# Encoder block on one core: five buffer and order edits between its stages

## The chip, the core and the metric

The program runs on one core of one Trainium2 chip. The time is device time of one execution in microseconds (us); of several runs the median is given. The engines are TensorE (PE; its weight loads are listed apart as PEld), VectorE (DVE), ScalarE (ACT), GpSimd (POOL) and SyncE (SP). SP, ACT and POOL also issue DMAs, each through its own queue. Each engine works through its instructions in a fixed order and stands still at an instruction whose inputs or buffers are not ready.

## What is computed

One layer of a bidirectional encoder, applied to a request of 256 tokens and to one of 512, with the same weights, all in float32, model width 1024. Cut to what matters:

```python
h = rmsnorm(x)
u, q, k, v, qm, gl = split(h @ w_in)               # 8192 columns
A = z * sigmoid(z @ s5_w_glu)                      # z = gelu(forward + backward S5 scan of u + d * u)
B = diff_attention(q, k, v)                        # 8 heads, two softmax maps each, rotary, norms
C = memory_attention(qm, rmsnorm(mem))             # 4 heads, 256 memory tokens
merged = sum_n sigmoid(gl_n + b_n) * (branch_n @ w_branch_n)    # n = A, B, C
x = x + merged @ w_out
x = x + (silu(g) * up) @ w_down                    # g, up = rmsnorm(x) @ w_gate_up
```

## The kernel before

All 768 tokens are worked on together. A stage's activations lie in SBUF with the features on the partitions, as a pair of float32r tiles, a high part and the residual, and so do the weights. A product is three matmuls into one PSUM bank (`mm3`, L748 to L753: high by high, high by residual, residual by high), for 8 slices k of the inner width. `dense_fm` (L755) runs this for 128 output features and one of the two token segments `SEGS`, 256 or 512 tokens wide; `between`, if given, is called after each k.

Weights come as a stream (`WStream`, L504): each chunk of 256 output columns is loaded in two halves into three raw buffers (`wr`, pool `W.praw`) by SP, ACT rounds it to the high part `wh` (L595), and DVE subtracts for the residual `wl` (L601); in some stages ACT writes the negated raw values (L598) and an accumulating DMA from POOL adds (L599).

**Who sets the order.** The program is written as one sequence. A planner then orders each engine's instructions ahead of time, by program order among what its own time estimates hold for ready, and places the tiles. `pin` (`keep_in_program_order`) puts an instruction behind everything written before it for its engine. `issue_after(ins)` puts what a block writes for the engine of `ins` behind `ins` in that engine's order. A pool's tiles with one tag share `bufs` buffers; a pool opened where a closed one lay waits, tile by tile, for the last use of what lay there. Side work is written as generators that `Pace` (L802) steps by a rate as the main loop calls `tick`.

The stages, in order, with what the change touches:

- *Memory keys, values and queries* with the memory attention beside them; its outputs go to DRAM (`mo_scr`).
- *u* (`u_chunk`, L1063): 4 chunks of 256 features. Each of the two 128-feature halves m gets a tile `ut` (three border columns are cleared by POOL, L277), filled by DVE for the 256-token segment (L1075) and ACT for the 512-token one (L1073), and stored to DRAM by SP (L282). Chunks 2 and 3 use a pool of one buffer (L1090), while DVE and ACT prepare the S5 parameters.
- *Gate logits* (L1105): 12 chunks of 256. ACT copies each result with its bias (L1114), SP stores it (L1115). Beside it the S5 scan runs as a generator, `s5.steps` (L452), 16 quads of 4 groups, each in several steps: `build` (DVE products, and ACT copies L310), `response`, `weights` (transposes L357 with ACT copies L358), `tables` (12 ACT instructions L375 to L377, then sines), `states` (products L403, DVE L391 to L426) and `outputs`. There are two PSUM banks for the gate logits.
- *Queries, keys and values* of the differential attention (L1392): units of 128 tokens, 24 matmuls of 256 columns each, with the gelu of the S5 outputs (`gelu`, L1366) and `diff_attend` (L1246) beside. `stack(h, i)` (L1213) transposes head h's queries (i = 0) or keys (i = 1): two groups of transposes into the three banks of `env.psb`, copied out by ACT (L1232) and DVE (L1234, L1236); for the keys two DMAs from POOL follow (L1240). In the last units POOL loads the memory branch's input over the normed activations, in three thirds of 256 tokens (L1404).
- *Branch C* (`branch(2, ...)`, L1491, called at L1544): 4 chunks of 256 features, two halves m each. A gate tile is loaded by POOL (L1499) and goes through tanh on ACT (L1500); DVE multiplies it with each segment's result (L1506). The rest of the attention is stepped between the k slices. At chunk 3 (`tail`, L1532) the attention is drained, its pools are closed, and `x1` and then the z pair (L1540) are placed where they lay; `load_pair` (L1521) splits the stored z into the pair, ACT L745 and DVE L746. The last head's output tile `do` is filled by ACT (L1334) and stored from ACT's queue (L1335).
- *Half-GLU* (L1547), then branches A and B, then `w_out`.
- *Feed-forward*: gate and up blocks by a seven-product scheme with half-size operands, and the down projection likewise (L1695 on): products in the order P2, P1, P5, P6, P3, P7, P4, each of 6 granules g, 42 items. `w_fetch(i)` (L1731) loads a quarter of the down weights, in some products with an accumulating DMA from POOL behind it (L1754). `make(i)` (L1757) splits the weights (`whd` by ACT L742, `wld` by DVE L743), sums or subtracts two activation quarters on DVE (L1767; P5, P6, P3 and P7 only) and splits the result (`dxh` by ACT L745, `dxl` by DVE L746), all pinned. In iteration i the loop fetches item i + 6, makes item i + 2 and issues the 18 matmuls of item i; behind a product's last granule DVE adds the sums to `x1` (L1846).

## Time and profile before

| | |
|---|---|
| median of 3 runs | 1772.24 us |
| the runs | 1771.3 to 1774.49 us |
| the profiled execution | 1774.09 us |
| its span | 1772.3 us |
| mean granted TensorE clock | 0.997 |
| moved by DMA | 234.09 MB, mean 132 GB/s |

The profile's span runs from the first to the last instruction; about 1.8 us of the execution lie around it. "Busy" is the time in which an engine works on an instruction, weight loads listed apart. In the view of waits a row names the engine, operation and line that stood still, what released it, the total, the number of times and the longest. In the timeline a row has its start, its duration, engine, line, operation, output and inputs with their sizes, and in brackets how long the engine was idle before and what ended it. A row of the chain of waits has start, duration and what it was. In a table by stretches each stretch has its length, the busy time of PE, PEld, DVE, ACT and POOL, the granted TensorE clock, the busy share of the DMA engines and their GB/s.

```profile
PEclk9999999999999999999999999999999999999999
DMA  7223745655556456444773336331312323239765
```

These two rows give the span in 40 equal slices, in tenths: the granted clock, and the share in which the DMA engines are busy, high at the start and again near the end, in the down projection.

### The profile page before, as it was taken

Reading aid. Unit: us, or ns where it says so; the run is one execution under the profiler, and the core shown is the slowest. Engines: PE = TensorE matmul, PEld = TensorE weight load, DVE = VectorE, ACT = ScalarE, POOL = GpSimd, SP = SyncE. Lnnn points to the kernel's source line nnn. Section 1 sums busy time; section 2 is a strip of 40 time slices with the busy share of each in tenths; the row PEclk is TensorE's granted clock in tenths of the full one; section 3 lists DMA queues with packets and bytes.
Section 4 is the critical chain, followed back from the end, with each engine's and each line's share of the span. In section 5 each row is a group of like instructions: output and inputs, shape, how many; then the busy total and the mean of one; then the engine's idle time right before and its main releaser. Section 6 shows DMA issues by size and latency. Waiting matters only on the chain.

```text
span 1772.3 us, 29415 instructions
## 1 busy us (share of the span) xinstructions
PE 1743.5 (98%) x11194; PEld 1609.4 (91%) x11194; DVE 1268.0 (72%) x2349; ACT 887.5 (50%) x1856; POOL 277.0 (16%) x296
## 2 busy tenths in 40 slices
PE   9999999999999999999989999999999999999998
PEld 9999988999999999999979888888889999998876
DVE  6665659699999679788876435453598777776775
ACT  6445444676676356877766434232343333334333
POOL 0000000000000101110110002000036565641112
PEclk9999999999999999999999999999999999999999
DMA  7223745655556456444773336331312323239765
GB/s 266 73 84 98 141 111 120 175 129 146 146 141 159 130 151 172 107 97 95 158 174 103 119 125 238 121 116 60 92 58 90 117 86 114 90 125 284 191 159 120
DMA packets 209661, 234.09 MB, mean 132 GB/s; under 512 B 57832, under 2 KB 173296, under 8 KB 209520
## 3 DMA queue, kind: packets, MB, share of 16 engines
q1 hardware_dynamic: 184080, 164.05, 30.6%
q0 software_dynamic: 24288, 65.02, 17.1%
q10 hardware_dynamic: 1152, 3.15, 0.5%
q8 instruction: 88, 1.44, 0.3%
q14 instruction: 53, 0.43, 0.1%
HBM read 165.78 MB, written 41.22 MB: 117 GB/s over the span
## 4 chain that ended last, share of the span: by engine, by line
PE 57%; DMA 3%; DVE 2%; issue 1%; ACT 1%; POOL 0%; SPq 0%; ACTq 0%; POOLq 0%; DVEq 0%
PE br L751 3%; PE br L752 3%; PE br L753 3%; PE gate L751 3%; PE gate L753 3%; PE up L753 3%; PE gate L752 3%; PE up L752 3%; PE up L751 3%; PE dn L751 3%; PE dn L752 3%; PE dn L753 3%; PE av L1311 2%; PE qk L752 2%; PE qk L751 2%; PE qk L753 2%
## 5 line engine op out<-in xcount | busy, mean ns | idle before, releaser
L595 ACT ACTIVATE wh<-wr 128x1024 fp32r<-128x1024 f32 x124 | 140.6, 1134 | 75.7 <-PE br L752 31.0
L601 DVE TENSOR_TENSOR wl<-wr,wh 128x1024 fp32r<-128x1024 f32 x82 | 108.4, 1324 | 84.7 <-ACT wh L595 82.9
L751 PE MATMUL gl<-Hhi,wh 128*128 128x256 f32 (+1 forms) x384 | 133.1, 346 | 2.4 <-ACT glt L1114 2.4
L753 PE MATMUL gl<-Hhi,wl 128*128 128x256 f32 (+1 forms) x384 | 129.7, 338 | 0.0
L752 PE MATMUL gl<-Hlo,wh 128*128 128x256 f32 (+1 forms) x384 | 129.4, 337 | 0.0
L751 PE MATMUL qk<-wh,Hhi 128*128 128x256 f32 x384 | 108.8, 283 | 0.7 <-ACT V L1210 0.7
L752 PE MATMUL qk<-wl,Hhi 128*128 128x256 f32 x384 | 109.4, 285 | 0.0
L753 PE MATMUL qk<-wh,Hlo 128*128 128x256 f32 x384 | 108.6, 283 | 0.0
L599 POOL DMA_DIRECT2D wl<-wr x42 | 36.6, 872 | 455.5 <-ACT wl L598 428.6
L751 PE MATMUL dn<-whd,dxh 128*128 128x512 f32 x231 | 89.2, 392 | 4.8 <-ACT dxh L745 4.8
L752 PE MATMUL dn<-wld,dxh 128*128 128x512 f32 x231 | 88.7, 390 | 0.0
L753 PE MATMUL dn<-whd,dxl 128*128 128x512 f32 x231 | 82.0, 390 | 0.6 <-DVE dxl L746 0.6
L751 PEld LDWEIGHTS gl<-Hhi,wh 128*128 128x128 f32 x384 | 73.0, 190 | 9.8 <-ACT glt L1114 2.8
L753 PEld LDWEIGHTS gl<-Hhi,wl 128*128 128x128 f32 x384 | 72.7, 189 | 7.9
L752 PEld LDWEIGHTS gl<-Hlo,wh 128*128 128x128 f32 x384 | 73.1, 190 | 7.2
L1280 DVE TENSOR_REDUCE nm<-sc 128x1 f32<-128x512 f32 (+1 forms) x96 | 56.5, 597 | 26.2 <-PE sc L1275 25.3
L751 PEld LDWEIGHTS qk<-wh,Hhi 128*128 128x128 f32 x384 | 73.2, 191 | 1.6 <-ACT V L1210 0.9
L557 ACT ACTIVATE wh_S<-ws 128x512 fp32r<-128x512 f32 x70 | 41.1, 625 | 65.5 <-PE up L752 36.9
L753 PEld LDWEIGHTS qk<-wh,Hlo 128*128 128x128 f32 x384 | 73.5, 191 | 0.3
L752 PEld LDWEIGHTS qk<-wl,Hhi 128*128 128x128 f32 x384 | 73.0, 190 | 0.6
L558 DVE TENSOR_TENSOR wl_S<-ws,wh_S 128x512 fp32r<-128x512 f32 x70 | 57.9, 850 | 15.9 <-ACT wh_S L557 15.9
L1282 ACT ACTIVATE p<-sc,nm 128x512 f32<-128x512 f32 (+1 forms) x96 | 59.0, 619 | 17.4 <-DVE nm L1280 17.0
(480 smaller groups left out, 6001.4 us busy)
## 6 DMA issues: line engine op xcount, KB each, us to landing
wr<-in_w_in_dram SPq DMA_DIRECT2D x48, 512.0 KB, 4.6
wr<-in_w_gate_up_dram SPq DMA_DIRECT2D x44, 512.0 KB, 3.5
wl<-wr POOLq DMA_DIRECT2D x42, 512.0 KB, 5.1
wr<-in_w_branch_dram SPq DMA_DIRECT2D x24, 512.0 KB, 4.2
glr<-gl_scr POOLq DMA_DIRECT2D x24, 384.0 KB, 3.5
hid_scr<-fa SPq DMA_DIRECT2D x11, 768.0 KB, 6.3
wr<-in_w_mem_kv_dram SPq DMA_DIRECT2D x16, 512.0 KB, 3.6
wr<-in_w_in_dram SPq DMA_DIRECT2D x32, 256.0 KB, 4.4
```

What stands on the lines that cost most here:

```text
L557: self.nc.scalar.activation(f(hi), src, AF.Copy)
L558: self.nc.vector.tensor_tensor(out=f(lo), in0=src, in1=f(hi).bitcast(F32), op=ALU.subtract)
L595: self.nc.scalar.activation(hi, r, AF.Copy)
L599: self.nc.gpsimd.dma_start(lo, r.bitcast(F32R), accum_op=ALU.add)
L601: self.sub.tensor_tensor(out=lo, in0=r, in1=hi.bitcast(F32), op=ALU.subtract)
L751: pe.matmul(ps, wh, xh, start=start, stop=False, **kw)
L752: pe.matmul(ps, wh, xl, start=False, stop=False, **kw)
L753: pe.matmul(ps, wl, xh, start=False, stop=stop, **kw)
L1280: v.tensor_reduce(out=nm[:, m : m + 1], in_=ps, axis=AX.X, op=ALU.max, negate=True)
L1282: act.activation(pm[:, 0:n], ps, AF.Exp, bias=nm[:, m : m + 1], accum_out=s1s[:, tt : tt + 1] if m == 0 else s2)
L1311: pe.matmul(po[:, 0:128], aT[:, 128 * k : 128 * k + 128], V[:, c0 // 128 + k, 128 * (h % 2) : 128 * (h % 2) + 128], start=(k == 0), stop=( ...
```

## The change

The edits do not change what is computed. In the order of the program:

- *u*: in chunks 2 and 3 the first half m keeps its one-buffer pool, the second gets one of its own, placed behind a filler of 9372 floats.
- *Gate logits*: for M = 2 and 3 (chunk 1), the S5 steps that the tick issues are put behind the gate copy (L1114) in ACT's order.
- *Heads' buffer*: a tile of the tag `do` is taken at once when the attention's pool opens, so that this buffer comes first in the pool.
- *First head*: the second stack is issued one step after the first, with one empty step less behind it.
- *First branch chunk*: for chunk 0 of branch C both gate tiles are loaded first, and the tokens are taken by thirds: 0 to 255 for both halves, then 256 to 511 for both, then 512 to 767 for both, the last two into one bank per half.
- *Half-GLU*: for chunk 0 the four results (two halves, two segments) are run together, k by k, in four banks, one of them from the pool `a`.
- *Down parts*: `make` sums first, then ACT splits weights and activations one after the other, then DVE takes both residuals. The raw weights of P3 and P7 alternate between the three buffers `dwt` and the three of the weight stream; before, P3 used only the latter and P7 only the former.

```diff
@@ -736,14 +736,14 @@
     def mean_eps(x, n, d):
         v.tensor_scalar(out=x, in0=x, scalar1=1.0 / d, scalar2=1e-6, op0=mul, op1=add)
 
-    def split_evac(hi, lo, src, scale=None, pin=lambda i: i):
+    def split_evac(hi, lo, src, scale=None):
 
         if scale is None:
-            pin(act.activation(hi, src, AF.Copy))
-            pin(v.tensor_tensor(out=lo, in0=src, in1=hi.bitcast(F32), op=sub))
+            act.activation(hi, src, AF.Copy)
+            v.tensor_tensor(out=lo, in0=src, in1=hi.bitcast(F32), op=sub)
         else:
-            pin(act.activation(hi, src, AF.Copy, scale=scale))
-            pin(v.scalar_tensor_tensor(out=lo, in0=src, scalar=scale, in1=hi.bitcast(F32), op0=mul, op1=sub))
+            act.activation(hi, src, AF.Copy, scale=scale)
+            v.scalar_tensor_tensor(out=lo, in0=src, scalar=scale, in1=hi.bitcast(F32), op0=mul, op1=sub)
 
     def mm3(ps, wh, wl, xh, xl, start, stop, more=False):
 
@@ -1060,10 +1060,10 @@
     uctx = ExitStack()
     up = uctx.enter_context(tc.tile_pool(name="utp", bufs=2))
 
-    def u_chunk(c, tick):
+    def u_chunk(c, tick, pools=None):
         w = W.get()
         for m in range(2):
-            ut = s5.u_tile(up, 2 * c + m)
+            ut = s5.u_tile(pools[m] if pools else up, 2 * c + m)
             for sg, (c0, n) in enumerate(SEGS):
                 ps = psd("u")
                 dense_fm(ps, w, m, H, c0, n)
@@ -1092,8 +1092,10 @@
 
         gap.tile([128, 512], F32, name="s5gap")
         s5.params(scr, env.psb)
-        u_chunk(2, lambda w: None)
-        u_chunk(3, lambda w: None)
+        with tc.tile_pool(name="utgap", bufs=1) as gap2, tc.tile_pool(name="utp3", bufs=1) as up3:
+            gap2.tile([128, 9372], F32, name="utgap")
+            for c in (2, 3):
+                u_chunk(c, lambda w: None, (up, up3))
     uctx.close()
 
 
@@ -1111,9 +1113,10 @@
                     gt = glp.tile([128, 512], F32, name=uid("glt"), tag="glt")
                     ps = psd("gl")
                     dense_fm(ps, w, m, H, c0, n)
-                    act.activation(gt[:, 0:n], ps[:, 0:n], AF.Identity, bias=bg[:, M : M + 1])
+                    out = act.activation(gt[:, 0:n], ps[:, 0:n], AF.Identity, bias=bg[:, M : M + 1])
                     nc.sync.dma_start(gl_scr[M][:, c0 : c0 + n], gt[:, 0:n])
-                    pace.tick(1.0 + sg)
+                    with tc.issue_after(out.ins) if M in (2, 3) else ExitStack():
+                        pace.tick(1.0 + sg)
         pace.drain()
     psum(2, a=2, b=3, d=3)
     s5ctx.close()
@@ -1129,6 +1132,7 @@
     tC = q1.tile([128, 4, 4, 64], F32, name="ropeC")
     tS = q1.tile([128, 4, 4, 64], F32, name="ropeS")
     nlam = k1.tile([128, 1], F32, name="nlam")
+    k2.tile([128, TOK], F32, name="do_", tag="do", bufs=1)
 
     rp = q1.tile([128, TILES, 256], F32, name="ropesrc", tag="ropet")
     tab, lv = (rp[:, t].rearrange("p (t c) -> p t c", c=64) for t in range(2))
@@ -1248,8 +1252,9 @@
         while 0 not in RO:
             yield
         stack(0, 0)
+        yield
         stack(0, 1)
-        for _ in range(3):
+        for _ in range(2):
             yield
         N = 8 * TILES
         X = {}
@@ -1493,21 +1498,47 @@
                 if hook:
                     hook(c)
                 w = W.get()
+
+                def gate(m):
+                    g = gtp.tile([128, TOK], F32, name=uid("glr"), tag="glr")
+                    gp.dma_start(g, gl_scr[8 * n_ + 2 * c + m])
+                    act.activation(g, g, AF.Tanh, scale=0.5)
+                    return g
+
+                def merge(m, g, ps, c0, n):
+                    M = 2 * c + m
+                    dst = merged[:, M, c0 : c0 + n] if first else g[:, c0 : c0 + n]
+                    v.scalar_tensor_tensor(out=dst, in0=g[:, c0 : c0 + n], scalar=1.0, in1=ps[:, 0:n],
+                                           op0=add, op1=mul)
+                    if not first:
+                        v.tensor_tensor(out=merged[:, M, c0 : c0 + n], in0=merged[:, M, c0 : c0 + n],
+                                        in1=dst, op=add)
+
+                if first and c == 0:
+
+                    gs = [gate(m) for m in range(2)]
+                    between = lambda: tick(1.0 / 8)
+                    for m in range(2):
+                        ps = psd("br")
+                        dense_fm(ps, w, m, X, 0, 256, between=between)
+                        merge(m, gs[m], ps, 0, 256)
+                        between()
+                    pss = [psd("br") for _ in range(2)]
+                    for o in (0, 256):
+                        for m in range(2):
+                            dense_fm(pss[m][:, o : o + 256], w, m, X, 256 + o, 256, between=between)
+                            between()
+                    for m in range(2):
+                        merge(m, gs[m], pss[m], 256, 512)
+                    continue
                 for m in range(2):
                     M = 2 * c + m
-                    g = gtp.tile([128, TOK], F32, name=uid("glr"), tag="glr")
-                    gp.dma_start(g, gl_scr[8 * n_ + M])
-                    act.activation(g, g, AF.Tanh, scale=0.5)
+                    g = gate(m)
                     for sg, (c0, n) in enumerate(SEGS):
                         ps = psd("br")
                         between = tick and (lambda: tick((1.0 + sg) / 8))
                         dense_fm(ps, w, m, X, c0, n, between=between)
-                        dst = merged[:, M, c0 : c0 + n] if first else g[:, c0 : c0 + n]
-                        v.scalar_tensor_tensor(out=dst, in0=g[:, c0 : c0 + n], scalar=1.0, in1=ps[:, 0:n],
-                                               op0=add, op1=mul)
-                        if not first:
-                            v.tensor_tensor(out=merged[:, M, c0 : c0 + n], in0=merged[:, M, c0 : c0 + n],
-                                            in1=dst, op=add)
+                        merge(m, g, ps, c0, n)
                         if tick:
                             between()
                     if MG:
@@ -1546,14 +1577,24 @@
         S = pair(XA, "s5o")
         for c in range(4):
             w = W.get()
+            if c == 0:
+                pss = {(0, 0): psd("glu"), (0, 1): psd("glu"), (1, 0): psd("glu"), (1, 1): env.psa("glu")}
+                for k in range(8):
+                    for (m, sg), ps in pss.items():
+                        c0, n = SEGS[sg]
+                        mm3(ps[:, 0:n], *w(k, 128 * m, 128), Z[0][:, k, c0 : c0 + n], Z[1][:, k, c0 : c0 + n],
+                            k == 0, k == 7)
             for m in range(2):
                 M = 2 * c + m
                 t = gtp.tile([128, TOK], F32, name=uid("gt"), tag="glr")
                 zs = stg.tile([128, TOK], F32, name=uid("zs"), tag="brr")
                 gp.dma_start(zs, z_scr[M])
-                for c0, n in SEGS:
-                    ps = psd("glu")
-                    dense_fm(ps, w, m, Z, c0, n)
+                for sg, (c0, n) in enumerate(SEGS):
+                    if c:
+                        ps = psd("glu")
+                        dense_fm(ps, w, m, Z, c0, n)
+                    else:
+                        ps = pss[m, sg]
                     act.activation(t[:, c0 : c0 + n], ps[:, 0:n], AF.Tanh, scale=0.5)
                 v.scalar_tensor_tensor(out=t, in0=t, scalar=1.0, in1=zs, op0=add, op1=mul)
                 split_evac(S[0][:, M], S[1][:, M], t, 0.25)
@@ -1746,7 +1787,7 @@
                 acc = {P5: (0, 1), P6: (1, 1), P4: (1, 0)}[p]
             t = ch[g]
         else:
-            t = view(DP["r"].tile([128, 1024], F32, name=f"dwt{i}", tag="dwt") if p == P7 else
+            t = view(DP["r"].tile([128, 1024], F32, name=f"dwt{i}", tag="dwt") if p in (P3, P7) and i % 2 else
                      W.praw.tile([128, W.HALF], F32, name=f"dwr{i}", tag="wr"))
             src, acc = {P3: ((1, 1), None), P7: ((0, 1), (1, 1)), P2: ((1, 0), None)}[p]
             pin(nc.sync.dma_start(t, w_quarter(*src, g)))
@@ -1762,7 +1803,6 @@
         n = granule(0, g)[2]
         t = w_raw.pop(i)
         wh, wl = (x.rearrange("p (k c) -> p k c", k=2)[:, 0:n] for x in W.tiles(f"d{i}"))
-        split_evac(wh, wl, t, pin=pin)
         A_ = lambda r, kh: a_raw[(r, kh), g]
         tt = lambda o, x, y, op: pin(v.tensor_tensor(out=o, in0=x, in1=y, op=op))
         sign = 0.5
@@ -1785,7 +1825,10 @@
         else:
             x = A_(*((0, 1) if p == P2 else (1, 1)))
         xh, xl = (da_f.tile([128, 2, HT], F32R, name=uid("dx" + w), tag="dx" + w)[:, 0:n] for w in "hl")
-        split_evac(xh, xl, x, sign, pin)
+        pin(act.activation(wh, t, AF.Copy))
+        pin(act.activation(xh, x, AF.Copy, scale=sign))
+        pin(v.tensor_tensor(out=wl, in0=t, in1=wh.bitcast(F32), op=sub))
+        pin(v.scalar_tensor_tensor(out=xl, in0=x, scalar=sign, in1=xh.bitcast(F32), op0=mul, op1=sub))
         parts[i] = xh, xl, wh, wl
 
     def item_loads(i):
```

## The prediction, made before the result

> **What bounds the kernel now.** The page comes first.
>
> ```profile
> span 1772.3 us, 29415 instructions
> PE 1743.5 (98%) x11194; PEld 1609.4 (91%) x11194; DVE 1268.0 (72%) x2349; ACT 887.5 (50%) x1856; POOL 277.0 (16%) x296
> ```
>
> PE works 98% of the span, and the diff takes no matrix product away. So only the 1772.3 - 1743.5 = 28.8 us in which PE stands still can be won, and whatever time PE works at a lower clock. Next comes the view of PE's waits.
>
> ```profile
> PE dn L751 <- ACT dxh L745: 4.8, 4, 2.7
> PE br L752 <- DMA Hlo<-mo_scrl: 2.6, 1, 2.6
> PE gl L751 <- ACT glt L1114: 2.4, 1, 2.4
> PE glu L751 <- ACT zhi L745: 2.1, 1, 2.1
> PE qkT L1226 <- DVE qst L1236: 2.1, 1, 2.1
> PE sc L1274 <- ACT p L1282: 1.4, 2, 1.2
> ...
> PE u L751 <- DVE ut L1075: 1.1, 1, 1.1
> PE br L751 <- DMA Hhi<-mo_scrh: 1.0, 1, 1.0
> PE qk L751 <- ACT V L1210: 0.7, 1, 0.7
> ...
> PE sc L1274 <- DMA kst<-kst: 0.7, 1, 0.7
> PE dn L753 <- DVE dxl L746: 0.6, 1, 0.6
> ```
>
> Each row is one place: who waited, for whom, the total, how often, the longest. Five places hold nearly all that lies between start and end: the u chunks with the first gate logits (1.1 + 2.4), the first head's transposes (2.1), the first branch chunk (2.6 + 1.0, then 1.4 of scores), the half-GLU (2.1) and the down projection (4.8 + 0.6). The third view is the granted clock in short stretches behind such stops (column before the last two: 1.00 is full).
>
> ```profile
> 308.00:312.00 4.00, 4.00 (x24) 3.92 (x23) 3.97 (x8) 2.72 (x8) 0.00 (x0) 0.65 1.01 256
> 666.00:670.00 4.00, 4.00 (x24) 4.00 (x23) 3.88 (x8) 3.06 (x8) 0.55 (x1) 0.60 0.57 136
> 1004.00:1008.00 4.00, 3.87 (x16) 3.35 (x16) 3.70 (x5) 2.17 (x3) 1.61 (x3) 0.61 0.87 283
> 1740.00:1744.00 4.00, 4.00 (x19) 3.29 (x18) 2.93 (x5) 2.54 (x4) 0.00 (x0) 1.00 1.12 205
> ```
>
> PE counts as busy in all four, but behind three stops (gl, qkT, glu) the clock is cut: 4 x 0.35 = 1.4 us, 4 x 0.40 = 1.6 us and 4 x 0.39 = 1.6 us of work lost beside the stop. Behind the longest stop (2.7, in the down part) it is not.
>
> [...]
>
> **The change part by part.** Everything is summed against the profiled execution, 1774.09 us (span 1772.3 and 1.8 around it), which stands 1.85 us above the median of the three runs shown, 1772.24.
>
> *Two u tiles, and S5 work queued behind the gate copies.*
>
> ```profile
> 289.75 0.18 POOL L277 MEMSET ut<- 128x8 f32 x3 [11.60 <-DMA u_scr<-ut]
> 300.14 0.38 ACT L375 ACTIVATE w<-s5kpos,s5v 128x99 f32<-128x99 f32 x1
> 306.12 1.03 ACT L1114 ACTIVATE glt<-gl,bg 128x256 f32<-128x256 f32 x2
> 339.64 0.98 DVE L391 TENSOR_TENSOR X<-psI,cs 128x792 f32<-128x792 f32 x1 [4.51 <-PE psI L403]
> 677.62 0.12 PE qk L751
> 1246.93 0.47 PE wo L752 x2
> ```
>
> The last two rows are the pitch of PE: 0.12 us for a product of 256 columns, 0.47 / 2 = 0.235 for one of 512; an m of 24 and 24 takes 8.5. With one u tile in chunks 2 and 3, the next tile's memset sits behind the store of the last (289.75), the copies out of PSUM behind the memset, and PE behind the copies: 1.1 us. With two in turn, a tile is wanted again only a whole m later; the stop goes. The gate stop is ACT's order: table work (L375) for the first S5 quad runs from 300.14, while the first gate copy, whose PSUM bank PE wants back, comes at 306.12. The order edges put all that the steps of M = 2 and 3 issue on ACT (bpad copies, tables, copies of E transposed) behind the gate copies of M = 2 and 3; their DVE, PE and SP instructions are not tied. So the gate copy of M = 0 has only u copies, weight splits and the first quad's bpad ahead: 2.4 + 1.4 us of clock. The price: the tables now start behind the second gate copy of M = 2, three m of 8.5 us behind the gates' start instead of a little after it, so some 20 us later, about 320, and they need 6 us or more (300.14 to 306.12, among other work). Their first user is the DVE product at 339.64, which moves ahead by the 4.9 us won. That leaves a few us; I take no cost here (ends: 0, and the rival on the S5 stage below). **4.9 us** (ends 0 and 4.9).
>
> *One unit between the two stacks.*
>
> ```profile
> 658.88 5.36 DMA y<-y_scr
> 671.22 0.59 ACT L1232 ACTIVATE kst<-qkT 64x512 fp32r<-64x512 f32 x1
> 672.11 4.96 DMA kst<-kst
> ```
>
> Four transposes' groups share three PSUM banks, so the fourth waits for the first to be copied out, on ACT and DVE queues that stand in order behind the gelu work, itself late by its y load. The added yield moves the second stack (transposes, copies, and two kst DMAs on POOL) one unit later and drops one yield behind it, so the scores keep their place. The fourth group then need not wait (2.1). But its kst copy, today at 671.22, and the 4.96 us DMA cannot come earlier for it, and PE reaches the scores earlier; the 0.7 us wait on kst can grow by what was won. Ends: 0 and 2.1 + 1.6 + 0.7 = 4.4. I take the middle, nearest to the stop itself, and leave the clock out: **2.1 us**.
>
> *First branch chunk by thirds.*
>
> ```profile
> 895.94 12.93 DMA Hlo<-mo_scrl
> L752 PE MATMUL br<-Hlo,wh x128: 276/379/483, 894.8 to 1000.5; 128*128 128x256 f32 x64, 128*128 128x512 f32 x64
> ```
>
> The last third of the memory branch's input lands at 895.94 + 12.93 = 908.9. Today PE needs it after 24 products of 256 columns. By thirds it does 96 products on the first two thirds first: 96 x 0.12 = 11.5 us, beside as much attention as the ticks give. The branch started just before 894.8, so it asks after 906 even with no attention between; the attention work, now 1/8 tick per k throughout, carries it past 909. Cut smaller, the products cost the same, twice 0.12 for 0.235. The stops 2.6 + 1.0 go. The 1.4 (and 0.2 more, from the rows between) of scores waiting for their exponentials stood in a run of attention that PE did while it had no branch work; with branch work between it goes too. New: both gate tiles are held to the chunk's end, so the next gate load on POOL waits there, and kst DMAs behind it in that queue; the next chunk's first merge is three PSUM banks away (about 11 us of PE), more than load and tanh, so nothing. **5.2 us** (ends 2.6 and 5.2).
>
> *Heads' buffer lower, half-GLU over four banks.*
>
> ```profile
> 999.58 2.71 DMA br_scr<-do
> 1000.97 1.06 ACT L595 ACTIVATE wh<-wr 128x1024 fp32r<-128x1024 f32 x1 [1.42 <-PE br L752]
> 1002.39 0.84 ACT L745 ACTIVATE zhi<-brr 128x768 fp32r<-128x768 f32 x1 [0.37 <-DMA br_scr<-do]
> ```
>
> The z pair lies on the last head's output buffer, so its first split waits for that buffer's store (until 1002.3). With the buffer first in its pool, under x1's later place, this wait goes; next in line are the attention tiles' last reads, ahead of that store's start at 999.58, and ACT's order. If the split stands ahead of the weight split at 1000.97, z is ready before PE ends the branch. Four banks make a k step 6 x 0.12 + 6 x 0.235 = 2.1 us of PE against 0.84 us of ACT per z tile, so PE cannot outrun the splits. The four results end one behind the other within the last k step, and each bank is copied out while the next ends. Stop and clock: 2.1 + 1.6 = **3.7 us** (ends 0, if ACT's order keeps the weight split first, and 3.7).
>
> *Down parts and raw buffers.*
>
> ```profile
> 1698.82 1.04 ACT L742 ACTIVATE whd<-dwr 128x1024 fp32r<-128x1024 f32 x1
> 1702.10 0.85 ACT L745 ACTIVATE dxh<-ds 128x768 fp32r<-128x768 f32 x1 [2.24 <-DVE ds L1767]
> 1721.16 6.97 DMA dwt<-in_w_down_dram
> 1728.70 6.35 DMA dwt<-in_w_down_dram
> 1735.14 1.06 ACT L742 ACTIVATE whd<-dwt 128x1024 fp32r<-128x1024 f32 x1 [2.97 <-DMA dwt<-in_w_down_dram]
> ```
>
> Today ACT idles 2.24 us in every item, because the second ACT copy needs a DVE sum that DVE does behind the weight residual. One item takes 1702.10 + 0.85 - 1698.82 = 4.1 us, the 18 x 0.235 = 4.2 us that PE takes: no reserve, so the x additions at a product's end show up as stops. In the new order DVE sums first, and both ACT copies follow each other; the item is then DVE's alone, about 3.1 us (the 2.24 that ACT waits for residual and sum, and some 0.9, as long as ACT's copy of the same tile, for the last). A microsecond an item refills the reserve of two items. The last stops are loads: P7's weights take a load and an accumulating load in turn (6.35 us the second) from three buffers, each asked for only when three items earlier is split. With six, the load asks six items ahead with its buffer long free, SP and POOL do not stand on it, and it has 4 x 4.2 = 16.8 us where two loads of 7.0 and 6.35 us need 13.4. All of it: 4.8 + 0.6 = **5.4 us** (ends 2.0 and 5.4).
>
> *New waits.* The order of every engine is planned anew. Handovers that nobody tuned show 0.7 us each (the qk row of the waits); I charge five: **3.5 us** (ends 0 and 8).
>
> Sum: 4.9 + 2.1 + 5.2 + 3.7 + 5.4 - 3.5 = 17.8 us. 1774.09 - 17.8 = 1756.3 on the profiled execution's scale, 1754.4 on the median's.
>
> [...]
>
> **The rivals.** *Stops that move.* The waits of PE are only the last in a chain of in-order queues. If the gate copy still stands behind other ACT work, the kst load takes the stack's gain, and the z split stays behind the weight split, then only 1.1 + 0 + 3.6 + 0 + 5.4 = 10.1 remains, less 2 of new waits: 1764. For: in the chain of waits the y load at 658.88 and the kst copy and DMA up to 677 stand in a row, not PE. Against: the diff removes the named cause at each place.
>
> *S5 held back: slower.*
>
> ```profile
> 450.00:500.00 50.00, 50.00 (x345) 46.01 (x344) 48.55 (x68) 33.89 (x86) 1.90 (x3) 1.00 0.60 154
> 603.27 0.98 DVE L391 TENSOR_TENSOR X<-psI,cs 128x792 f32<-128x792 f32 x1 [5.24 <-PE psI L403]
> ```
>
> In mid-stage DVE works 48.55 of 50 us, and PE's order has S5 products among the gate products. If the delayed tables start the 16 quads late, DVE cannot catch up, and PE can stop p us in each. Then the first term is gone: 16.4 - 3.5 = 12.9 won, 16 p lost; slower than today by 0.2% from p = (12.9 + 3.5) / 16 = 1.0 us on. At p = 1.5: 1772.2 - 12.9 + 24 = 1783. Against: at the end DVE waits 5.24 us for PE, so it has reserve.
>
> *The edit does not bite* (another tile still under the z pair, the same order planned again, new waits of 8): about 1770.
>
> [...]
>
> **How the numbers follow.** Forecast 1754.4 (1748 to 1760): 0.55. Stops that move, 1764 (1760 to 1768): 0.24. The clock rule, 1757: 0.05. Not biting, 1770: 0.06. Slower, 1783: 0.07. Better than all terms, under 1748: 0.03. About 0.2%, 3.5 us, is what a measurement here tells from no change. Faster by more: 0.55 + 0.24 + 0.05 + 0.03 = 0.87; within: 0.06; slower: 0.07. The range 1747 to 1767 leaves out the slower case, no change, and a tail on each side: under 0.2.
>
> **What would show it.** Right: PE's idle time falls from 28.8 to about 12; the rows gl, br, glu and dn leave the waits; clock 1.00 near 305 and 1000; ACT's 2.24 us before dxh gone. Wrong: a psI, psK or psE row among PE's waits; kst above 2 us; zhi behind L595. What I know least is how the planner orders ACT around the stacks and z splits.

## The result, and the profile after

The changed kernel takes 1764.95 us (median of 6 runs, 1764.09 to 1765.39) against 1772.34 us (6 runs, 1771.3 to 1774.49): a ratio of 0.9956, 95% interval 0.9944 to 0.9969. That is 7.4 us less, where 17.8 were forecast. Its profiled execution took 1765.39 us. In a later set of runs the same kernel took 1766.03 us against 1776.4 (0.9939, 0.9927 to 0.9951).

The page after, its span and the busy time of PE:

```profile
span 1763.6 us, 29524 instructions
PE 1740.1 (99%) x11242; PEld 1611.4 (91%) x11242; DVE 1267.4 (72%) x2349; ACT 889.0 (50%) x1856; POOL 276.0 (16%) x296
```

PE stands still for 23.5 us instead of 28.8; about 12 were forecast. The view of PE's waits says where (who waited, for whom, total, times, longest):

```profile
PE sc L1279 <- DMA kst<-kst: 4.3, 2, 2.8
PE psK L326 <- DMA wr<-in_w_in_dram: 2.8, 1, 2.8
PE glu L751 <- ACT zhi L745: 2.2, 1, 2.2
PE qkT L1230 <- DVE qst L1240: 2.1, 2, 1.7
...
PE sc L1279 <- ACT p L1287: 0.6, 2, 0.3
```

The rows of dn, gl, u and of the branch's input are gone, as forecast. A psK row is new, the kst row has grown from 0.7 to 4.3, and the glu row is what it was. (The releaser named in the psK row, a weight load, is inferred; the cause is shown below.) The clock, in stretches of 3.41 us (busy time, granted clock in the column after the count):

```profile
313.43:316.84 3.41, 0.59 (x4) 1.00 1.07 324
316.84:320.26 3.42, 3.42 (x17) 0.50 0.65 163
675.24:678.65 3.41, 0.59 (x5) 1.00 1.23 264
678.65:682.06 3.41, 3.41 (x17) 0.50 0.83 258
999.51:1002.92 3.41, 1.94 (x9) 1.00 0.65 199
1002.92:1006.33 3.41, 2.69 (x14) 1.00 0.65 221
```

Half clock follows the two new stops; behind the half-GLU, whose stop is as long as before, it is gone. (Below, a stop that half clock follows is called cut.)

Where the time went is read best from PE's own timeline: take the same product in two profiles and subtract. The table gives what each stretch gained (-) or lost (+) against the first profile of before, in us. Its ends are the first u product (211.17 before), the first query product (611.41), the end of the last v (894.86), the end of the last score (973.74), the first wo (1205.70), the first dn (1603.65) and the end of the last dn (1768.20).

| stretch | forecast | after | after, 2nd profile | before, 2nd profile |
|---|---|---|---|---|
| start | 0 | +1.64 | +1.11 | +1.32 |
| u, gate logits, S5 | -4.9 | -1.05 | -0.43 | -0.71 |
| queries, keys, values, first scores | -2.1 | +2.09 | +1.78 | +0.75 |
| branch C with attention | -5.2 | -2.40 | -2.10 | +1.86 |
| end of branch C, half-GLU, other branches | -3.7 | -1.72 | -1.17 | -0.72 |
| wo, gate, up | 0 | +0.01 | +0.01 | 0.00 |
| down | -5.4 | -7.27 | -7.27 | +0.01 |
| new waits, anywhere | +3.5 | | | |
| sum | -17.8 | -8.70 | -8.07 | +2.51 |

The last column is the unchanged kernel: stretches differ by 1 to 2 us between two executions of one program. The runs show why (clock grid, last section). The down part is what was hoped for and more; the stacks lost what they should have won; three stretches gave a fifth to a half of their terms.

### The profile page after: what moved, and what is told of

It reads as the page before. It is cut to its first block, busy times and chain, and to the rows that moved or that the text cites. A ratio compares the mean times of both kernels' runs of the same rounds, so it can differ in the third digit from the quotient of the medians.

```text
span 1763.6 us, 29524 instructions
## 1 busy us (share of the span) xinstructions
PE 1740.1 (99%) x11242; PEld 1611.4 (91%) x11242; DVE 1267.4 (72%) x2349; ACT 889.0 (50%) x1856; POOL 276.0 (16%) x296
## 4 chain that ended last, share of the span: by engine, by line
PE 59%; DMA 2%; issue 1%; DVE 1%; ACT 1%; POOL 0%; SPq 0%; DVEq 0%; ACTq 0%; POOLq 0%
PE br L752 4%; PE br L751 4%; PE br L753 4%; PE gate L751 3%; PE up L751 3%; PE gate L753 3%; PE up L752 3%; PE gate L752 3%; PE up L753 3%; PE dn L752 3%; PE dn L753 3%; PE dn L751 3%; PE av L1316 2%; PE qk L752 2%; PE qk L753 2%; PE qk L751 2%
## 5 line engine op out<-in xcount | busy, mean ns | idle before, releaser
L595 ACT ACTIVATE wh<-wr 128x1024 fp32r<-128x1024 f32 x124 | 140.6, 1134 | 69.1 <-PE br L752 28.3
L753 PE MATMUL dn<-whd,dxl 128*128 128x512 f32 x231 | 88.9, 389 | 0.0
```

The costliest lines, as they stand in the source:

```text
L595: self.nc.scalar.activation(hi, r, AF.Copy)
L753: pe.matmul(ps, wl, xh, start=False, stop=stop, **kw)
```

## The experiments

My theory after the result, in three parts: a closed pool is waited for *as a whole* (so the second u tile holds up S5, and a lower place inside the same pool frees nothing); the stack's yield and the third loads make the key stack's DMA late; and half clock comes from a grid that the kernel doesn't control. The main rivals were that the order on ACT, or full DMA engines, set these places.

The old kernel took 1772.3 to 1776.4 us in the four sets of runs, so each ratio is against the old kernel run beside it, and what one place gained is read from the stretches of the table, in the profiled execution.

### a_s5pool: two S5 tiles in a pool of their own

```diff
         self.pq = ctx.enter_context(self.tc.tile_pool(name="s5q", bufs=1))
+        self.pr = ctx.enter_context(self.tc.tile_pool(name="s5r", bufs=1))
...
-        new = lambda tag, bufs: pq.tile(B3, ...)
+        new = lambda tag, bufs: (self.pr if tag == "W" else pq).tile(B3, ...)
...
-        Ysb = pq.tile(
+        Ysb = self.pr.tile(
```

> The kernel after, with the S5 work tiles W and Ysb in a pool of their own above the rest, so that the pool of G, E and the others no longer lies over the third u tile. Theory (a pool waits as a whole): the first G product, at 308.35 in the profile after, waited 9.04 us for the store of a u tile only because the two pools share addresses; it goes back to about 299, the 2.83 us stop before psK and the half clock behind it (another 1.5) go, and the time falls from 1765.0 by 3 to 4.6, to about 1761. Rival (the order edges): G is late because the S5 steps of the first gate products were tied behind the gate copies; G stays near 308, psK's stop stays, the time stays at 1765.

Measured: 1762.52 us (0.9921, 0.9908 to 0.9933). The first G product in DVE's timeline, in the kernel after and here:

```profile
308.35 1.23 DVE L293 TENSOR_TENSOR G<-s5C,s5Ar 128x1024 f32<-128x1024 f32 x1 [9.04 <-DMA u_scr<-ut]
```

```profile
299.35 1.23 DVE L294 TENSOR_TENSOR G<-s5C,s5Ar 128x1024 f32<-128x1024 f32 x1
```

The stretch of u, gates and S5 gains 5.00 us instead of 1.05, and psK's stop falls to 0.37. G itself lies at the bottom of the S5 pool; only W and Ysb, at its top, lie over the u tile. So the wait belongs to the pool, not to the tile. The theory holds; the rival falls. The time fell by less than the 3 to 4.6 us that were expected. (Of the 4 us won in the stretch, 1.1 were given back at the half-GLU, whose stop was cut in this execution and not in the one of after.)

### b_zown: the heads' buffer in another pool

```diff
-    k2.tile([128, TOK], F32, name="do_", tag="do", bufs=1)
...
-            do = k2.tile([128, TOK], F32, name=uid("do"), tag="do", bufs=1)
+            do = k1.tile([128, TOK], F32, name=uid("do"), tag="do")
```

> The kernel after, with the heads' output buffer taken out of the pool of the attention tiles and put into the pool below it, which the z pair does not touch. Theory (a pool waits as a whole): the lower place inside the same pool could not help, and the first z split still waited for that buffer's store; now it stands ahead of the weight split on ACT, near 999 instead of 1002.7, PE's stop before the half-GLU falls from 2.15 us to under 0.5, and the time falls by about 2.2, to 1762.8. Rival (ACT's order decides, my recorded lower end): the weight split stays first, the z split comes only 0.4 earlier, and the time falls by no more than 0.4.

Measured: 1760.4 us (0.9918, 0.9905 to 0.9932). ACT's timeline at the z splits, after and here:

```profile
1001.25 1.06 ACT L595 ACTIVATE wh<-wr 128x1024 fp32r<-128x1024 f32 x1 [1.41 <-PE br L752]
1002.71 1.58 ACT L745 ACTIVATE zhi<-brr 128x768 fp32r<-128x768 f32 x2 [0.40 <-DMA br_scr<-do]
```

```profile
997.52 0.84 ACT L745 ACTIVATE zhi<-brr 128x768 fp32r<-128x768 f32 x1
997.67 0.33 ACTq L1339 DMA_DIRECT2D br_scr<-do  x1
998.26 3.05 ACT L745 ACTIVATE zhi<-brr 128x768 fp32r<-128x768 f32 x4
1001.20 1.05 ACT L595 ACTIVATE wh<-wr 128x1024 fp32r<-128x1024 f32 x1
```

In the kernel after the buffer lies under x1 and no longer under z, and the first z split still waits for its store. In a pool that z does not touch, the wait is gone, the planner puts five z splits ahead of the weight split, and PE has no stop there at all: the stretch gains 4.50 us instead of 1.72. (The profiled execution is 5.0 us shorter than that of after; 2.8 of them lie here, 1.6 at the start.) The order on ACT, my recorded lower end, was a consequence of the same wait.

### c_stack_undo: the two stacks together again

```diff
         stack(0, 0)
-        yield
         stack(0, 1)
-        for _ in range(2):
+        for _ in range(3):
```

> The kernel after, with the two stacks of the first head put together again as before (no unit between them, three behind). Theory (the stop moved): the yield moved the second stack's copies and its loads later while PE came to the scores no later, so that the kst stop (2.82 us) and the half clock behind it cost more than the qkT stop saved; undone, kst falls to about 0.7, the qkT stop comes back at about 2.1, and the time falls by 1 to 2, to about 1763.5. Rival (the yield is worth what was forecast and the loss there comes from the shifted gelu work alone): the time rises by up to 2, to 1767.

Measured: 1764.85 us (0.994, 0.9927 to 0.9952). The score product that waits for the key stack, in PE's timeline, after and here:

```profile
678.48 0.44 PE L1279 MATMUL sc<-kst,qst 128*128 128x256 f32 x1 [2.82 <-DMA kst<-kst]
```

```profile
675.40 0.39 PE L1278 MATMUL sc<-kst,qst 128*128 128x256 f32 x1 [0.45 <-DMA kst<-kst]
```

The qkT stop is back at 2.10 (1.70 after), kst's falls to 0.45, and the stretch loses 0.61 us instead of 2.09. For the stops the theory holds. The price in time, 1.5 us in this pair, is less sure: in the seven profiles that have the yield and the S5 pool of after, the stretch lost 0.56 to 2.09 us (0.56 in e_dn_order_undo), in the three without the yield (before twice, and this one) 0, 0.75 and 0.61. So none of them shows the forecast gain of 2.1, and what the yield cost is about 1 us by the means, with ranges that overlap. The total shows none of it, because a 2.09 us stop near 909 was cut in this execution (its stretch gained 0.16 instead of 2.40).

### d_kst_act: the key stack's DMA on ACT's queue

```diff
-                gp.dma_start(T[m][o], T[m][s])
+                act.dma_start(T[m][o].bitcast(F32), T[m][s].bitcast(F32))
```

> The kernel after, with the second half of each head's key stack copied by a DMA that ACT issues, not POOL. Theory (the queue): the load waited at 911.7 took 12.2 us because it stood in POOL's queue behind the last third of the memory branch's input; on ACT's queue it lands in about 3 us, as the store that ACT issues near 1000 does (2.7), both kst stops (2.82 and 1.52) fall below 0.7, and the time falls by 3 to 5, to about 1761. Rival (the DMA engines are full there, share 0.86 to 1.11): the load takes as long on any queue and the stops stay within 0.5 us, time 1765; or the issues cost ACT more than they save, time above 1766.

Measured: 1764.92 us (0.994, 0.9928 to 0.9952). POOL's timeline of after shows the load (L1244) behind the branch's last third; the row below it, from the DMA view between 895 and 912, has its size and its time to landing:

```profile
897.72 0.91 POOL L1409 DMA_DIRECT2D Hhi<-mo_scrh  x1 [4.16 <-PE v L753]
898.62 0.88 POOL L1409 DMA_DIRECT2D Hlo<-mo_scrl  x1
899.49 0.54 POOL L1244 DMA_DIRECT2D kst<-kst  x1
...
kst<-kst POOLq DMA_DIRECT2D x1, 192.0 KB, 12.2
```

The same here:

```profile
896.93 0.88 POOL L1409 DMA_DIRECT2D Hhi<-mo_scrh  x1 [6.76 <-PE v L753]
897.16 0.47 ACTq L1244 DMA_DIRECT2D kst<-kst  x1
897.80 0.88 POOL L1409 DMA_DIRECT2D Hlo<-mo_scrl  x1
...
kst<-kst ACTq DMA_DIRECT2D x1, 192.0 KB, 2.8
```

Half right. Near 910 the load lands in 2.8 us instead of 12.2, PE's stop of 1.52 is gone, and the stretch gains 4.13 instead of 2.40. But the rival, full DMA engines, is not ruled out: from ACT's queue the load was also issued 2.3 us sooner, between the two loads of 1024 KB instead of behind both, and while it ran the engines moved 152 GB/s, against 305 in the 12.2 us of after. The load before it, of the same size and issued some 2.6 us behind the loads of the second third, took 6.7 us from POOL's queue and 6.5 from ACT's: behind large loads ACT's queue was no faster. At the first head it did not help either: the load took 5.6 us (median of two) on ACT's queue, and PE still stopped for 1.27 and 2.69. The half-GLU's 2.14 us stop was cut in this execution, which hides the gain in the total.

### r_after: the changed kernel once more

> The kernel after once more, unchanged. In the profiles so far half clock comes in pieces of 3.41 us, and within each execution their starts lie on one grid of 3.41 us; a piece follows when PE stood still for 1.93 us or more of the 3.41 before it, and not when it stood still for 1.84 or less. Theory (a free-running grid): the stops stay where they are to 0.1 us, but the grid lies elsewhere, so that the 2.15 us stop before the half-GLU, the start and the two stops of 2.8 us may change places between cut and not cut; with each cut the rest of the execution moves by 1.3 to 1.6 us. The time stays at 1765 to 1768 with a spread of 1 to 3 us between executions. Rival (each stop has its own fixed answer): the clock is cut behind the same stops as in the first profile, psK, kst and the start, and not behind the half-GLU.

Measured: 1766.03 us (0.9939, 0.9927 to 0.9951), spread 1763.32 to 1766.71. The grid lay almost as in the first profile, so this run did not tell the theories apart: the same stops were cut. Stops repeated to 0.3 us, not to 0.1 (psK 3.08 against 2.83). The 1.84 of the expectation does not hold at the start: in the first profile of after, 1.56 us of idleness in the step from 9.64 were followed by half clock.

### e_dn_order_undo and f_dn_buf_undo: half of the down edit each

```diff
+        pin(act.activation(wh, t, AF.Copy))
+        pin(v.tensor_tensor(out=wl, in0=t, in1=wh.bitcast(F32), op=sub))
         A_ = lambda r, kh: a_raw[(r, kh), g]
...
-        pin(act.activation(wh, t, AF.Copy))
         pin(act.activation(xh, x, AF.Copy, scale=sign))
-        pin(v.tensor_tensor(out=wl, in0=t, in1=wh.bitcast(F32), op=sub))
```

> The kernel after, with the order of the copies in a down part put back (weight split first, then the sums, then the split of the sum), the six raw buffers kept. Theory (my recorded split of the term): buffers alone remove the two stops that a late load ended (0.72 and 2.75), the order removes the others (1.15, 0.16, 0.58, each with 0.27 of refilling); with the old order PE stops again in the last 70 us for 1.9 to 2.7 us in all and ACT again idles 2.2 us ahead of each split of a sum; the time rises by 2 to 2.7. Rival (the loads were all of it): no stop returns, the time does not change.

```diff
-            t = view(DP["r"].tile(...) if p in (P3, P7) and i % 2 else
+            t = view(DP["r"].tile(...) if p == P7 else
```

> The kernel after, with the raw buffers of the down parts put back (three for the second and third product kinds, separate ones for the seventh only), the new order of the copies kept. Theory (two causes side by side): the stops that a late load ended come back near the end, 0.72 and 2.75 with 0.27 of refilling each, so the time rises by 3 to 4. Rival (the order alone gives enough reserve, since an item is split earlier and so its buffer is free earlier): less than 1 us of stop comes back.

Measured: 1767.54 us for the old order (0.9954, 0.9941 to 0.9966), 1764.97 us for the old buffers (0.9939, 0.9926 to 0.9952). PE's waits with the old order:

```profile
PE dn L751 <- ACT dxh L1830: 1.3, 2, 1.1
...
PE dn L753 <- DVE dxl L1831: 0.5, 1, 0.5
```

These are before's first three down stops, and the down stretch gains 4.05 instead of 7.27. With the new order and the old buffers no down stop comes back: 7.27. So buffers alone are worth 4.05, the order alone all 7.27: my "two causes side by side" falls, the rival holds. An item that is split earlier also frees its buffer earlier; the six buffers are not needed.

### g_s5pool_no_issue: without the order edges

```diff
-                    with tc.issue_after(out.ins) if M in (2, 3) else ExitStack():
-                        pace.tick(1.0 + sg)
+                    pace.tick(1.0 + sg)
```

(on top of a_s5pool)

> The kernel with the S5 tiles W and Ysb in a pool of their own, without the order edges that tie the S5 work of the second and third gate products behind the gate copies. Theory (the edges removed the gate stop): the table work stands ahead of a gate copy on ACT again, PE stops for 1.5 to 2.4 us near 304, mostly with half clock behind it, and the time is 2 to 4 us above that of the same kernel with the edges (1762.5). Rival (the second u tile removed it, by letting the u copies run earlier): no stop near 304, and the time equals that of the kernel with the edges.

Measured: 1764.63 us (0.9939, 0.9925 to 0.9952). ACT's timeline, first and last of twelve table copies for one quad, and the gate copy behind them:

```profile
300.59 0.38 ACT L376 ACTIVATE w<-s5kpos,s5v 128x99 f32<-128x99 f32 x1
...
306.30 0.37 ACT L378 ACTIVATE R<-s5kmask,s5rho 128x99 f32<-128x99 f32 x1
306.56 1.03 ACT L1117 ACTIVATE glt<-gl,bg 128x256 f32<-128x256 f32 x2
```

PE stops for 3.35 us at 303.7 and two pieces of half clock follow; the stretch loses 0.66 instead of gaining 5.00. The edges do what the forecast said, and the delayed tables cost nothing: no psI or psE wait shows in any profile.

### k_zown_two_banks: the half-GLU's first chunk as before

```diff
-            if c == 0:
+            if c < 0:
                 pss = {(0, 0): psd("glu"), ...}
```

(and the results taken as in the other chunks; on top of b_zown)

> The kernel after with the heads' output buffer in the pool below, and the half-GLU's first chunk one result after the other again, as before. Theory (the recorded step: four banks let PE take 2.1 us a k step, two z splits of 0.84 and 0.96 in 1.1 us apiece cannot keep up with 0.7 us a step of a single result of 256 columns): without the four banks PE waits for split after split, 1 to 3 us of stops in the first 10 us of the half-GLU, time 1 to 3 above that of the kernel with only the buffer moved (1760.4). Rival (with the first split 3 us earlier the splits have reserve): no stop, the same time.

Measured: 1761.84 us (0.993, 0.9918 to 0.9942). The start of the half-GLU in the windows view (busy time second):

```profile
1000.45:1011.50 11.05, 11.05 (x71) 1.00 0.88 274
```

No stop: the stretch gains 4.50, as with four banks. The rival holds; PE's order runs both segments' results side by side anyway, and with the first split early that is slow enough. Four banks are worth nothing here.

### i_best and j_best_kst: the mends together

i_best joins the edits of a, b and c; j_best_kst also issues the key stacks' DMAs from ACT, save for the first head.

> Three mends together: the S5 tiles W and Ysb in a pool of their own, the heads' output buffer in the pool below the attention tiles, the two stacks together as before. Theory (the terms add at their places): against the kernel after, 3.9 us less at the start of S5, 2.8 less at the half-GLU, 1.5 less at the stacks; 1765 to 1766 becomes about 1758, less or more by 1.5 with every cut of the clock that falls otherwise. Rival (the gain goes on to the next stop): PE comes to the stacks some 4 us earlier while the gelu chain ahead of them does not, so that the qkT, kst and score stops grow by 3 or more and the time stays near 1761.

> The same three mends, and the key stacks' DMAs issued by ACT for all heads but the first (the first keeps POOL, since there the DMA from ACT's queue landed no sooner). Theory: the kst stop near 910 (1.36 to 2.33 in the runs so far) goes, with any half clock behind it, and the time is 1.5 to 2.5 below the kernel with three mends, about 1756. Rival: what PE wins there is waited for at the scores behind it (the exponentials and the sums of DVE), and the time is the same within 0.5.

Measured: 1758.3 us (0.9898, 0.9885 to 0.9911) and 1755.87 us (0.9892, 0.9879 to 0.9905). PE's waits in the second:

```profile
PE qkT L1230 <- DVE qst L1240: 3.3, 2, 2.9
PE sc L1281 <- ACT p L1289: 2.6, 3, 2.0
PE sc L1281 <- DMA kst<-kst: 2.0, 1, 2.0
```

i_best gains 4.94 in the S5 stretch, 2.34 in the branch and 4.20 at the half-GLU, but loses 1.48 at the stacks: PE begins the queries at 608.29 instead of 612.00, while the second key DMA is issued at 672.12 (673.67 in after, 670.69 in c_stack_undo), so qkT (3.13) and kst (2.06) are waited for longer. Theory for the first three, rival for the fourth. In j_best_kst the kst stop near 910 is gone. The medians differ by 2.4, as expected, but the executions of the two kernels overlap (1754.86 to 1758.69 against 1755.18 to 1756.84), and most of the difference between the two profiled ones, 1.7 of 1.9 us, lies at the start. The branch's stretch is 0.8 shorter, with one further piece of half clock in it.

### r_before: the old kernel once more

> The kernel before, unchanged, for a second profile. Theory (the grid of 3.41 us): its stops are those of the first profile to 0.1 us; the three cuts (gl, qkT, half-GLU) need not be the same ones, and the stops of 2.59 and 2.75 us (the branch's last third, the last down part) can be followed by half clock here, with 1.3 to 1.6 us more of time for each cut. Rival (other reasons for the difference between sets of runs): the same three cuts and no other.

Measured: 1773.86 us (12 runs, 1771.29 to 1779.36; 0.9997, 0.9988 to 1.0005). Its cuts were at the start, behind u, qkT, the branch's last third and the half-GLU; the first profile's were behind gl, qkT and the half-GLU. The branch's stop is the cleanest pair: 2.59 us without a cut in the first profile, 2.63 us with one here. The part "stops repeat to 0.1 us" held for most, not for u and gl (1.91 and 0.73 here, 1.06 and 2.41 there).

## Why the prediction was wrong, step by step

- **Two u tiles and the order edges** (forecast -4.9, came -1.05). Both sub-steps were right: the u stop and the gate stop went (the edges: g). The step that failed is "I take no cost here": I looked for the late party among the tables, and it was G, held until 308.35 by the second u tile's store, because that tile's pool lies under the S5 pool. psK then stopped 2.83 us with half clock behind it. With the pool parted the term measures 5.00.
- **One unit between the stacks** (forecast -2.1, came +2.09). "The fourth group then need not wait" failed: the qkT stop stayed at 1.70 of 2.10, and at 1.66 to 1.70 in every profile with the yield and the S5 pool of after. And the kst wait grew from 0.66 to 2.82. I had written that the kst copy and its DMA could not come earlier and that this wait could grow by what was won, and took the middle of the range all the same. Counted from the first query product, PE came to that score 1.4 us sooner (63.65 against 65.04) and the DMA landed 0.8 later (66.43 against 65.66). The sign was wrong; undone, the stretch stands at +0.61.
- **First branch chunk by thirds** (forecast -5.2, came -2.40). The waits for the input went. Mis-sized were two parts. The key load behind the last third's loads in POOL's queue, which I had noticed only for gate tiles, stopped PE for 1.52 us in their place; in the kernel before it was as late (12.8 us to landing), hidden behind PE's stop for the input. And the attention's waits stayed (0.35, 0.45, 0.23 and 0.40 against 1.19, 0.23 and 0.17); no run shows why branch work between them did not help.
- **Heads' buffer and four banks** (forecast -3.7, came -1.72). "With the buffer first in its pool this wait goes" failed: pools are waited for whole, and the statement in the description above that a pool waits tile by tile for what lay there is wrong in these places. The stop stayed at 2.15. What came is the clock term alone, by chance: a grid line at 1002.92 parted the stop (1.47 us of idleness in the step before it, 0.72 in the step behind). In another pool the term measures 4.50; the four banks add nothing.
- **Down** (forecast -5.4, came -7.27). Right in mechanism, small in size. ACT's timeline after shows the item at 2.87 us (1697.47 less 1694.60; 3.1 was estimated, and it was 4.03 before, 1702.10 less 1698.07):

```profile
1694.60 0.85 ACT L1829 ACTIVATE dxh<-ds 128x768 fp32r<-128x768 f32 x1 [2.80 <-DVE ds L1807]
1695.35 1.05 ACT L1828 ACTIVATE whd<-dwt 128x1024 fp32r<-128x1024 f32 x1
1697.47 0.85 ACT L1829 ACTIVATE dxh<-ds 128x768 fp32r<-128x768 f32 x1 [1.07 <-DVE ds L1807]
```

  ACT's idle time between an item's two copies did not go, as I had written: it fell from 2.24 to 1.07, and what ends it is still the sum on DVE. DVE, which had stood still for 1.00 in each item until ACT had written dxh, now works without a pause and sets the pace. Its timeline before and after:

```profile
1702.98 0.96 DVE L746 SCALAR_TENSOR_TENSOR dxl<-ds,dxh 128x768 fp32r<-128x768 f32 x1 [1.00 <-ACT dxh L745]
```

```profile
1698.40 0.96 DVE L1831 SCALAR_TENSOR_TENSOR dxl<-ds,dxh 128x768 fp32r<-128x768 f32 x1
```

  The missing 1.9 us is time that is lost beside the stops and that the waits don't count. PE's timeline of before at its last stop:

```profile
1739.34 0.50 PE L751 MATMUL dn<-whd,dxh 128*128 128x512 f32 x1 [2.75 <-ACT dxh L745]
1739.67 0.39 PE L752 MATMUL dn<-wld,dxh 128*128 128x512 f32 x1
```

  The product before began at 1736.20, 3.14 us earlier: 2.91 over the pitch of 0.23, not 2.75; and the next comes after 0.33, another 0.10 over. With such rows about 0.27 us a stop are lost beside the wait, 1.3 us for five stops; the rest are shorter slips of the same kind (0.10 to 0.23) that show no wait at all.
- **New waits** (forecast +3.5): the new stops are psK (2.83 and a cut) and the growth of kst at two places (from 0.66 to 4.34 in all). That is 6.5 us at three places, where five handovers of 0.7 were charged: a different thing, and nearly twice the amount, though inside the ends of 0 and 8.
- **The rivals.** *Stops that move*, 1764 at a chance of 0.24, is what happened, with two of its three conditions (the kst load, the z split). That its number came so near is luck in part: the stacks lost 2.09 where it had 0, and the down part gave 7.27 where it had 5.4. The S5 stage was not held back beyond its start. *The clock rule*, 1757 at a chance of 0.05, in which the clock terms of 1.4 and 1.6 stay lost although the stops go, is shown by no run: half clock followed stops of 2.1 to 2.4 us in the first profile of before (0.50 from 307.42, 665.82 and 1003.74), and where the half-GLU's stop was gone, in b_zown, the clock was 1.00 from 999.08 to 1011.50. Of my own signs of being wrong, three appeared in the first profile: a psK row, kst above 2 us, zhi behind L595.

The mended kernel's ratio, 0.9892, is near the forecast's 1754.4 / 1772.24 = 0.9899: most of the terms existed, but the change as made did not collect them. The nearness itself is luck in part: the mended kernel has no yield, its key loads go another way, and the down part gives 1.9 us more than forecast.

## What to carry to other kernels

Before counting a stop as won, look at where the planner puts every buffer that the change adds or moves, and which pools lie over the whole pool that held it: a wait that is tied to a pool does not go away by moving a tile within it. A stop that is removed in front of a chain that is late anyway (here the gelu chain and its loads) reappears at that chain (in i_best, which gained 4.94 us in the S5 stretch, qkT was waited for by 3.13 and kst by 2.06); give the gain only up to what the chain allows. Compare the same instruction's start in two profiles, stretch by stretch: totals of a few microseconds mix the change with where half clock happened to fall.

## What the runs showed of the hardware

**Half clock comes on a grid.** In the 14 profiles each piece of half clock before the last matmul lasted 3.40 to 3.42 us (two in a row once), and within an execution all pieces start a whole number of 3.413 us apart (in the first profile of before 307.42, 665.82 and 1003.74: 105 and 99 steps). Most of them follow a step in which PE stood still for long *within the step*: of the 28 steps with 1.93 us or more in the 14 profiles, 27 were followed by a piece. Pairs of neighbouring steps, busy time second, clock in the column after the count; first the branch's stop of 2.59 us in the first profile of before, which a grid line parts:

```profile
904.75:908.17 3.42, 1.66 (x15) 1.00 1.12 314
908.17:911.58 3.41, 2.58 (x11) 1.00 0.06 19
```

then the same stop (2.63) in the second profile of before, inside one step:

```profile
907.86:911.27 3.41, 0.78 (x4) 1.00 0.60 215
911.27:914.68 3.41, 3.41 (x10) 0.50 0.00 0
```

then the closest calls: f_dn_buf_undo at the half-GLU, c_stack_undo at psK, and i_best at qkT:

```profile
998.63:1002.04 3.41, 1.50 (x7) 1.00 0.79 239
1002.04:1005.45 3.41, 3.19 (x17) 1.00 0.73 213
```

```profile
312.45:315.86 3.41, 1.48 (x12) 1.00 0.97 258
315.86:319.27 3.41, 3.41 (x19) 0.50 0.67 163
```

```profile
662.36:665.77 3.41, 1.47 (x13) 1.00 0.27 43
665.77:669.18 3.41, 3.41 (x31) 1.00 0.72 189
```

Idle for 1.91 of 3.41 us: no cut there; 1.93: cut; 1.94: no cut. (1.91 behind u in the second profile of before was cut as well, so the line lies there, and idle time alone does not draw it sharply. In i_best the grid is counted from its one piece behind the start's stop, at 13.82.) The 1.94 is the one of the 28 that no piece followed; none with 1.65 to 1.90 was followed by one. The longest stop without one is 3.37 us, before qkT in a_s5pool: a grid line parts it into 1.60 and 1.77. Cut with less were steps at the start (1.50 to 1.64 idle, in seven profiles), one near 913 in j_best_kst (1.38), and one that was itself at half clock (1.25, in g_s5pool_no_issue); why the first two, no run here shows. What a cut costs is seen best at the start, which the change leaves alone: the first u product came 0.84 to 1.82 later than in the first profile of before in the seven profiles with a cut there, and 0.32 earlier to 0.32 later in the others. At the half-GLU, whose stop was 2.11 to 2.15 us long, the stretch of the changed kernel gained 1.15 to 1.79 in the six profiles without a cut there, 0.61 with one in a_s5pool, and lost 0.12 with one in d_kst_act. So this stop of 2.1 us cost clock in two of eight profiles and not in six, by its place on the grid, which shifted with what stood ahead and from one execution to the next (in after, the step from 999.51 held 1.47 us of idleness; in d_kst_act, the step from 998.35 held 2.14).

**A small load behind large ones.** The key load of 192 KB took 12.2 us from POOL's queue behind two loads of 1024 KB, and 2.8 us from ACT's queue when it was issued 2.3 us sooner, between the two. Behind both loads of the third before, a load of the same size took 6.7 us from POOL's queue and 6.5 from ACT's. So what shows is that it landed sooner, 2.8 us against 12.2, where it went ahead of the second large load; whether the queue or the busy engines held it behind them, no run here tells apart.
